# A two-layer hybrid decoder step: the builder orders its instructions by timeline simulation

## The chip, the core and the metric

The kernel runs as one program on one core of a Trainium2 chip. The core has five engines that each work through a fixed list of instructions in order: TensorE (PE; PEld is its weight load), VectorE (DVE), ScalarE (ACT), GpSimd (POOL) and SyncE (SP, which here only issues DMAs). An instruction whose semaphores have not come holds up everything behind it in its engine's list. The metric is the device time of one execution in microseconds (us).

## What is computed

The reference is one inference step of a 2-layer decoder trunk. A prompt of 1024 tokens and eight samples of 8 new tokens each share every weight (d_model 1024, float32).

```python
# layer 0
h = rmsnorm(x); z = h @ w_in0
ya = gated short convolution (conv3) of z[..., :1536]
yb = RWKV-7: token shift, data-dependent decay, delta-rule state update, a step per token
x = x + concat(ya, yb) @ w_out0;  x = x + swiglu(rmsnorm(x))
# layer 1
h = rmsnorm(x); z = h @ w_in1
yc = forgetting attention, causal, with per-token log forget gates; each sample also
     attends to 2048 past rows of a paged K/V cache (page_table)
yd = Mamba-2 SSD: causal conv, chunked scan, gated rmsnorm
x = x + concat(yc, yd) @ w_out1;  x = x + swiglu(rmsnorm(x));  y = rmsnorm(x)
```

The outputs are y and every new state (convolution rows, shift row, WKV state, K, V, log forget gates, SSD state).

## The kernel before

**Halves.** The 1088 tokens (64 of the samples, 1024 of the prompt) are worked in two halves: H0, the samples and the first half of the prompt (576 columns, cut into tiles of 320 and 256), and H1, the second half of the prompt (512 columns). Activations lie with features on partitions. For the last FFN they are regrouped as F0 and F1.

**Dense work.** Every large product is done in three passes to keep float32 accuracy: weight and activation are each split in a rounded high part and a low rest (wh, wl; hh, hl, or hidh, hidl inside the FFN), and `mm3` (L202) issues wh·hh (L204), wh·hl (L205) and wl·hh (L206) into one PSUM accumulator `acc`. `load_w` (L191) brings a weight tile: a DMA of 512 KB on ACT's queue into `wraw`, the cast to wh on ACT (L196), the subtraction to wl on POOL or DVE (L198).

**Side work.** Beside that run three chains of many small steps, each of which goes from PE to DVE, ACT or POOL and back: the RWKV recurrence (L521 to L840: the matmuls L622, L639, L693, L721 and others, many of them 32x32), the attention and decode, and the SSD scan (L1438, L1447). In decode (L1186) each tile of 512 KB of the K cache comes by 8 DMAs on SP's queue (L1245) with addresses taken from the page table, into one of 4 buffers `kv`; DVE transposes it (L1249, into `kt`) and 8 matmuls (L1254) use it. V tiles come by POOL (L1297, matmuls L1290).

**Recording order.** The generators of dense and side work are woven together while the program is recorded:

```python
weave(first(), m.recurrence(H0), RATE[0])    # first: short_conv(H0), project(H1), part of conv H1
weave(second(), m.recurrence(H1), RATE[1])   # second: output product and FFN of H0, layer 0
```

Then the pool of buffers of layer 0 (`m0`) is closed and that of layer 1 (`m1`) opened. The dense part of layer 1 for H0 (`m.dense`, with the gates L987 and their transposition `by_token`, L1061) is recorded, after it `third()` (FFN of H1, dense part of H1) and the FFN of F0, woven with `side` (attention, decode and SSD of H0, then attention and SSD of H1), and last the FFN of F1.

At the opening of `m1` the program loads the constants of layer 1 (L919, L172) and runs `past()` (L1074): the page table, a gather of the past log forget gates (L1088), their running sum on DVE (L1096, L1099), one small matmul over pages (L1101), the result written to DRAM (L1107) and its last column read back into `pcl` (L1109). `by_token` transposes the gates with the matmuls L1067 and L1071; L1067 waits for the DVE copy L1043, L1071 for the DVE subtraction L1046, which reads `pcl`. L919 waits for the buffers of `m0`, that is for L837, the last matmul of the recurrence.

**What sets the order on the chip.** The recorded order is not the executed one. The builder has a scheduler: a model of the machine that steps through time, and at each step gives each engine, of the instructions that its model says are ready, the one recorded first. The lists that come out are fixed; on the chip each engine follows its own list in order, with semaphores between engines. Semaphores, buffers and the number of instructions follow from the program and that order.

## Time and profile before

| | |
|---|---|
| time, median of 3 runs | 3342.44 us (3337.44 to 3342.83) |
| profiled execution | 3342.04 us, span 3340.3 us |
| granted TensorE clock, mean | 0.974 |
| PE busy | 3169.4 us, 95% |
| DVE, ACT, POOL busy | 1906.4, 1058.7, 834.7 us |
| DMA | 409.20 MB, mean 123 GB/s |

PE is busy nearly throughout. Its three dense passes (L204 to L206) make most of it. A PE that counts as busy can still wait between two pipelined matmuls, so the spacing of matmuls tells more than the busy share. The other engines have room on the average; the average runs over stretches that differ, from pure dense work (958 to 1250 us) to stretches where dense and side work alternate.

### The profile page before, as it was taken

Reading aid. Unit: us, or ns where it says so; the run is one execution under the profiler, and the core shown is the slowest. Engines: PE = TensorE matmul, PEld = TensorE weight load, DVE = VectorE, ACT = ScalarE, POOL = GpSimd, SP = SyncE. Lnnn points to the kernel's source line nnn. Section 1 sums busy time; section 2 is a strip of 40 time slices with the busy share of each in tenths; the row PEclk is TensorE's granted clock in tenths of the full one; section 3 lists DMA queues with packets and bytes.
Section 4 is the critical chain, followed back from the end, with each engine's and each line's share of the span. In section 5 each row is a group of like instructions: output and inputs, shape, how many; then the busy total and the mean of one; then the engine's idle time right before and its main releaser. Section 6 shows DMA issues by size and latency. Waiting matters only on the chain. (4 is left out here: it accounts for less than half of the span.)

```text
span 3340.3 us, 63263 instructions
## 1 busy us (share of the span) xinstructions
PE 3169.4 (95%) x25213; PEld 2666.9 (80%) x25213; DVE 1906.4 (57%) x3643; ACT 1058.7 (32%) x2083; POOL 834.7 (25%) x561
## 2 busy tenths in 40 slices
PE   7999999999999998999999998989999998999998
PEld 7887667777889997977677675766777776899998
DVE  6766646565544447556655457565545656554445
ACT  4333323332222223345322223332224553322222
POOL 4423333332333333301300103002010001333332
PEclk9999999999999998999999999999999999999999
DMA  5322333211122234544345656775554334232222
GB/s 178 116 59 79 87 96 118 73 59 56 51 66 83 83 108 148 191 151 135 108 135 163 199 154 213 240 221 175 172 171 138 113 110 135 87 105 81 83 83 78
DMA packets 238471, 409.20 MB, mean 123 GB/s; under 512 B 37632, under 2 KB 129664, under 8 KB 238176
## 3 DMA queue, kind: packets, MB, share of 16 engines
q10 hardware_dynamic: 63232, 218.80, 20.2%
q1 hardware_dynamic: 165584, 152.27, 15.4%
q0 software_dynamic: 9360, 34.08, 3.0%
q8 instruction: 199, 3.26, 0.4%
q14 instruction: 96, 0.79, 0.1%
HBM read 352.23 MB, written 52.81 MB: 121 GB/s over the span
## 5 line engine op out<-in xcount | busy, mean ns | idle before, releaser
L204 PE MATMUL acc<-hh,wh 128*128 128x320 f32 (+2 forms) x3720 | 1264.9, 341 | 17.6 <-ACT hh L218 14.7
L206 PE MATMUL acc<-hh,wl 128*128 128x320 f32 (+2 forms) x3720 | 1255.4, 338 | 7.4 <-POOL wl L198 6.5
L205 PE MATMUL acc<-hl,wh 128*128 128x320 f32 (+2 forms) x3720 | 1254.8, 338 | 7.2 <-DVE hl L219 5.4
L204 PEld LDWEIGHTS acc<-hh,wh 128*128 128x128 f32 x3720 | 712.3, 192 | 97.5 <-ACT hh L218 19.4
L198 POOL TENSOR_TENSOR wl<-wraw,wh 128x1024 fp32r<-128x1024 f32 x225 | 539.6, 2398 | 1000.6 <-ACT wh L196 924.7
L196 ACT CAST wh<-wraw 128x1024 fp32r<-128x1024 f32 (+1 forms) x398 | 416.0, 1045 | 1139.4 <-PE acc L205 1054.1
L206 PEld LDWEIGHTS acc<-hh,wl 128*128 128x128 f32 x3720 | 712.8, 192 | 74.7 <-issue 11.1
L205 PEld LDWEIGHTS acc<-hl,wh 128*128 128x128 f32 x3720 | 713.0, 192 | 72.1 <-DVE hl L219 9.1
L205 PE MATMUL acc<-hidl,wh 128*128 128x320 f32 (+2 forms) x1056 | 353.1, 335 | 0.6 <-DVE hidl L219 0.6
L893 DVE TENSOR_TENSOR x<-x,acc 128x320 f32<-128x320 f32 (+2 forms) x528 | 270.3, 527 | 139.1 <-PE acc L206 136.1
L206 PE MATMUL acc<-hidh,wl 128*128 128x320 f32 (+2 forms) x1056 | 349.5, 332 | 0.0
L204 PE MATMUL acc<-hidh,wh 128*128 128x320 f32 (+2 forms) x1056 | 348.9, 337 | 0.4 <-ACT hidh L218 0.4
L198 DVE TENSOR_TENSOR wl<-wraw,wh 128x1024 fp32r<-128x1024 f32 x173 | 210.9, 1219 | 145.3 <-ACT wh L196 143.2
L1297 POOL DMA_INDIRECT kv<-in_cv,vidx x64 | 75.5, 1180 | 628.8 <-DVE kt L1249 134.4
L204 PEld LDWEIGHTS acc<-hidh,wh 128*128 128x128 f32 x1056 | 198.7, 189 | 24.0 <-issue 4.2
L205 PEld LDWEIGHTS acc<-hidl,wh 128*128 128x128 f32 x1056 | 199.2, 189 | 19.1 <-issue 2.2
L206 PEld LDWEIGHTS acc<-hidh,wl 128*128 128x128 f32 x1056 | 199.5, 189 | 15.6 <-issue 1.4
L219 DVE TENSOR_TENSOR hidl<-ft,hidh 128x512 fp32r<-128x512 f32 (+2 forms) x148 | 178.7, 1207 | 55.9 <-ACT hidh L218 55.8
L881 DVE SCALAR_TENSOR_TENSOR ft<-ft,acc 128x320 f32<-128x320 f32 (+2 forms) x132 | 70.1, 531 | 213.1 <-PE acc L206 212.9
L875 DVE SCALAR_TENSOR_TENSOR ft<-ft,acc 128x320 f32<-128x320 f32 (+2 forms) x132 | 69.7, 528 | 177.0 <-ACT ft L874 176.8
L218 ACT CAST hidh<-ft 128x512 fp32r<-128x512 f32 (+2 forms) x148 | 75.1, 507 | 117.5 <-DVE ft L881 114.3
L1249 DVE STREAM_TRANSPOSE kt<-kv 128x1024 f32<-128x1024 f32 x64 | 79.3, 1239 | 33.8 <-DMA kv<-in_ck 29.9
(339 smaller groups left out, 3334.7 us busy)
## 6 DMA issues: line engine op xcount, KB each, us to landing
wraw<-in_wi ACTq DMA_DIRECT2D x100, 512.0 KB
wraw<-in_wg ACTq DMA_DIRECT2D x88, 512.0 KB
wraw<-in_wu ACTq DMA_DIRECT2D x88, 512.0 KB
wraw<-in_wd ACTq DMA_DIRECT2D x88, 512.0 KB
kv<-in_ck SPq DMA_DIRECT2D x512, 64.0 KB
wraw<-in_wo ACTq DMA_DIRECT2D x32, 512.0 KB
ka<-kp SPq DMA_DIRECT2D x48, 128.0 KB
x<-in_xT SPq DMA_DIRECT2D x16, 288.0 KB
```

Of the source, the lines that this page charges most:

```text
L196: nc.scalar.copy(wh, raw)
L198: k.low.tensor_sub(wl, raw, wh)
L204: mm(acc, wh, xh, start=first, stop=False)
L205: mm(acc, wh, xl, start=False, stop=False)
L206: mm(acc, wl, xh, start=False, stop=last)
L218: k.nc.scalar.copy(hh, v)
L219: (eng or k.nc.vector).tensor_sub(hl, v, hh)
L875: nc.vector.scalar_tensor_tensor(s[:, a:b], s[:, a:b], 1.0, pc, op0=ALU.add, op1=ALU.mult)
L881: nc.vector.scalar_tensor_tensor(s[:, a:b], s[:, a:b], 0.5, pu, op0=ALU.mult, op1=ALU.mult)
L893: nc.vector.tensor_add(xs[n][:, a:b], xs[n][:, a:b], acc[:, :b - a])
L1249: V.transpose(kt, kr)
L1297: nc.gpsimd.indirect_dma_start(out=v, out_offset=None, in_=A["cv"].rearrange("o (s r) c -> (o s) (r c)", r=2), in_offset=bass.IndirectOffs ...
```

## The change

One argument of the context in which the program is recorded:

```diff
-    with tile.TileContext(nc) as tc:
+    with tile.TileContext(nc, schedule_with_timeline_sim=True) as tc:
         hybrid_step(tc, A, O)
```

The scheduler takes another model of the machine, a timeline simulation, to decide which instruction is ready when. No operation is added or removed: there are 20191 matmuls in both programs, and 3643 instructions of DVE. What differs is where they stand in the lists of their engines. PE's list differs most; the start (to about 154 us of the trace), the FFN of H1 and the last FFN stand nearly as before. Three places follow.

**First recurrence, PE.** Before, at the matmul L639 that reads tile t0_3303 (recurrence of H0; t0 and wm are small 32x32 blocks of it, hh and wh the operands of the projection of H1):

```order
L639 MATMUL rk_3305<-t0_3303,nt_2877 32x32 x16
L204 MATMUL acc_3381<-hh_233,wh_3348 128x256
L205 MATMUL acc_3381<-hl_241,wh_3348 128x256
L206 MATMUL acc_3381<-hh_233,wl_3350 128x256
L204 MATMUL acc_3381<-hh_234,wh_3348 128x256
L639 MATMUL rk_3326<-t0_3324,nt_2889 32x32 x16
L205 MATMUL acc_3381<-hl_242,wh_3348 128x256
L206 MATMUL acc_3381<-hh_234,wl_3350 128x256
```

Now, at the same matmul:

```order
L563 MATMUL rk_3300<-sq_3298,con1_259 128x256
L206 MATMUL acc_6859<-hh_6481,wl_6829 128x256
L639 MATMUL rk_3305<-t0_3303,nt_2877 32x32 x16
L639 MATMUL rk_3326<-t0_3324,nt_2889 32x32 x16
L639 MATMUL rk_3407<-tt_3274,wm_3322 32x32 x16
L639 MATMUL rk_3426<-tt_3293,wm_3343 32x32 x16
L693 MATMUL rk_3453<-t0_3450,big_2772 32x32
L693 MATMUL rk_3453<-t0_3450,big_2854 32x32
```

Before, groups of recurrence matmuls and dense passes alternate to the end of the recurrence. Now the dense passes run ahead: the second row is the last of them, and behind it 1274 matmuls of the recurrence follow (376 rows of the list) with no dense pass among them, until the output product of H0 begins.

**Opening of layer 1, PE.** Before, the small matmul of `past()`, L1101 (ptot: totals of the log forget gates of a page), and, more than 500 rows further down, `by_token` (L1067, L1071):

```order
L204 MATMUL acc_15190<-hh_14791,wh_15185 128x320
L205 MATMUL acc_15190<-hl_14799,wh_15185 128x320
L1101 MATMUL rk_15041<-ptot_15039,con3_15016 128x8
L206 MATMUL acc_15190<-hh_14791,wl_15187 128x320
L204 MATMUL acc_15190<-hh_14792,wh_15185 128x320
```

```order
L205 MATMUL acc_15931<-hl_14802,wh_15900 128x256
L206 MATMUL acc_15931<-hh_14794,wl_15902 128x256
L1067 MATMUL acc_15959<-con0_222,x_15148 128x128 x4
L1071 MATMUL acc_15965<-con0_222,x_15148 128x128
L204 MATMUL acc_15978<-hh_14787,wh_15970 128x320
L205 MATMUL acc_15978<-hl_14795,wh_15970 128x320
```

Now the end of the recurrence of H1 (L820, L828, L837) and these matmuls stand together:

```order
L206 MATMUL acc_15931<-hh_14794,wl_15902 128x256
L820 MATMUL rk_11829<-con1_259,s2_11766 128x2 x2
L828 MATMUL rk_11836<-con0_222,s2_11766 128x128 x2
L837 MATMUL rk_11841<-sg_11761,g2_275 128x256
L1067 MATMUL acc_15959<-con0_222,x_15148 128x128 x4
L1101 MATMUL rk_15041<-ptot_15039,con3_15016 128x8
L1071 MATMUL acc_15965<-con0_222,x_15148 128x128
L204 MATMUL acc_15978<-hh_14787,wh_15970 128x320
```

Before, L837 stands some 2800 rows ahead of L1067, and dense passes lie between L1101 and L1067. Now nothing but these few small matmuls stands between L837 and L1071. On SP's list the loads of L919, L172, L1081 and on to L1109 follow directly on the last store of the recurrence, L840.

**Decode, PE.** Before, near the end of the dense part of H1 (kt: a transposed tile of K, qsp: queries; 8 matmuls L1254 use one tile):

```order
L205 MATMUL acc<-hl,wh 128x512
L206 MATMUL acc<-hh,wl 128x512
L1254 MATMUL fs<-kt,qsp 32x128 x8
L204 MATMUL acc<-hh,wh 128x512
L205 MATMUL acc<-hl,wh 128x512
L206 MATMUL acc<-hh,wl 128x512
L1263 MATMUL fs<-ksp,qsp 32x64 x8
L1254 MATMUL fs<-kt,qsp 32x128 x8
L204 MATMUL acc<-hh,wh 128x512
L205 MATMUL acc<-hl,wh 128x512
L206 MATMUL acc<-hh,wl 128x512
```

Now, at the same place of the dense work:

```order
L1311 MATMUL rk<-con_15016,om 64x16 x8
L1254 MATMUL fs<-kt,qsp 32x128 x64
L204 MATMUL acc<-hh,wh 128x512 x2
L205 MATMUL acc<-hl,wh 128x512
L206 MATMUL acc<-hh,wl 128x512
L205 MATMUL acc<-hl,wh 128x512
L206 MATMUL acc<-hh,wl 128x512
L1254 MATMUL fs<-kt,qsp 32x128 x40
L1263 MATMUL fs<-ksp,qsp 32x64 x8
L1254 MATMUL fs<-kt,qsp 32x128 x24
L204 MATMUL acc<-hh,wh 128x512 x2
```

Before, a K tile stands between three or more dense passes. Now 128 matmuls L1254, which is 16 K tiles, stand in a row with six dense passes among them. Before, the recurrence of H1 ends in the first half of the FFN of H0; now it is spread over the whole of it. At the end of the dense part of H1 the last 100 matmuls of the SSD scan of H1 (L1438, L1447 and others) now stand without dense passes as well.

## Rows read from the trace of the kernel before

**Rows 1.** The page: one engine's busy time, and the granted clock in 40 slices.
```profile
PE 3169.4 (95%) x25213; PEld 2666.9 (80%) x25213; DVE 1906.4 (57%) x3643; ACT 1058.7 (32%) x2083; POOL 834.7 (25%) x561
PEclk9999999999999998999999999999999999999999
```

**Rows 2.** Windows: stretch, its length, busy us (records) of each engine, clock, DMA.
```profile
core 0: us, PE busy (x) PEld busy (x) DVE busy (x) ACT busy (x) POOL busy (x), PEclk, DMA share, GB/s
154.00:528.00 374.00, 352.78 (x4702) 269.10 (x4700) 229.55 (x615) 119.43 (x321) 121.09 (x107) 0.96 0.30 87
528.00:958.00 430.00, 401.97 (x4937) 332.20 (x4938) 246.29 (x600) 129.26 (x319) 127.88 (x98) 0.96 0.20 63
958.00:1250.00 292.00, 292.00 (x2163) 289.78 (x2162) 125.37 (x217) 70.66 (x106) 108.20 (x45) 1.00 0.27 89
1520.00:1985.00 465.00, 452.95 (x2548) 335.71 (x2552) 278.39 (x461) 136.64 (x258) 62.93 (x68) 0.98 0.48 148
1985.00:2221.00 236.00, 220.60 (x1341) 160.17 (x1329) 150.49 (x199) 73.39 (x106) 32.30 (x26) 0.97 0.73 221
2221.00:2255.00 34.00, 26.19 (x142) 19.85 (x141) 17.79 (x23) 15.36 (x23) 1.82 (x4) 0.85 0.64 207
2742.00:2832.00 90.00, 79.84 (x414) 61.27 (x413) 63.80 (x133) 35.56 (x74) 16.18 (x11) 0.96 0.36 114
```

**Rows 3.** Waits of PE: us in total, times, longest us.
```profile
PE rk L639 <- DVE wm L660: 8.7, 6, 2.7
```

**Rows 4.** Windows of line L204 alone: length, PE busy (records), PEld, clock, DMA.
```profile
528.00:958.00 430.00, 167.64 (x505) 97.74 (x506) 0.96 0.20 63
254.00:279.00 25.00, 8.43 (x26) 4.88 (x26) 1.00 0.21 64
```

**Rows 5.** Lines by form, PE, 154 to 528 us: count, busy us, mean ns.
```profile
L204 PE MATMUL acc<-hh,wh 128*128 128x512 f32 x136 | 61.2, 450 | 0.0
```

**Rows 6.** Timeline of PE at 2245 us: start us, length us, instruction.
```profile
2244.93 0.39 PE L204 MATMUL acc<-hh,wh 128*128 128x512 f32 x1
2245.17 0.39 PE L205 MATMUL acc<-hl,wh 128*128 128x512 f32 x1
```

**Rows 7.** Windows of 25 us, columns as in rows 2.
```profile
154.00:179.00 25.00, 23.11 (x385) 20.44 (x384) 22.03 (x51) 8.30 (x19) 6.31 (x7) 0.93 0.18 51
254.00:279.00 25.00, 24.57 (x486) 19.83 (x487) 17.23 (x54) 7.63 (x24) 4.70 (x4) 1.00 0.21 64
```

**Rows 8.** Timeline, 1258 to 1370 us, the lines of past() and by_token().
```profile
1260.52 0.33 SPq L919 DMA_DIRECT2D st_conv<-in_st_conv  x1
...
1284.02 0.39 PE L1101 MATMUL rk<-ptot,con 128*128 128x8 f32 x2 [2.35 <-DVE ptot L1099]
1286.62 3.85 SPq L1107 DMA_DIRECT2D ncd<-plf  x8
...
1365.78 0.60 PE L1067 MATMUL acc<-con,x 128*128 128x128 f32 x4
```

**Rows 9.** One line, L1046: duration ns min/median/max, first and last start.
```profile
L1046 DVE TENSOR_TENSOR x<-x,pcl x1: 214/214/214, 1315.2 to 1315.2; 8x64 f32<-8x64 f32 x1
```

**Rows 10.** Timeline, 2139 to 2226 us: transposes of K tiles on DVE.
```profile
2139.60 1.25 DVE L1249 STREAM_TRANSPOSE kt<-kv 128x1024 f32<-128x1024 f32 x1 [6.34 <-DMA kv<-in_ck]
2143.62 1.25 DVE L1249 STREAM_TRANSPOSE kt<-kv 128x1024 f32<-128x1024 f32 x1 [1.01 <-DMA kv<-in_ck]
...
2224.02 1.24 DVE L1249 STREAM_TRANSPOSE kt<-kv 128x1024 f32<-128x1024 f32 x1
```

**Rows 11.** Timeline of SP, the same stretch: K loads.
```profile
2161.76 27.28 SPq L1245 DMA_DIRECT2D kv<-in_ck  x32
```

**Rows 12.** Chain of waits, 2815 to 2850 us: start us, us, what.
```profile
2822.49 1.17 PE rk L255 x8
...
2831.24 4.70 DMA ft<-yb
...
2836.01 0.68 ACT hh L218
```

## The prediction

> **What bounds the kernel now.** The page comes first. PE is busy 3169.4 of 3340.3 us and its granted clock stands near 1 in all slices [rows 1], so PE sets the time, and the change leaves PE's instructions as they are. What an order can change is how long PE waits, how long it runs at the lower of its two clock levels (1.2 against 2.4 GHz), and how long work of another engine lies with nothing for PE beside it. The windows by stage show how these differ now [rows 2]. From 958 to 1250 us PE has dense passes alone: 292.0 busy of 292 us, clock 1.00, 2163 matmuls, so 0.135 us for one of 320 or 256 columns. From 154 to 528 and from 528 to 958 us the two recurrences run beside dense work. There PE is idle 21.2 and 28.0 us and the clock is 0.96. The waits behind it are many and short: the longest sum of such a pair, L639 for wm, is 8.7 us in 6 times, none over 2.7 [rows 3]. The stretch 2221 to 2255, where the K tiles of decode get dense, is the worst by share: 7.8 of 34 us idle, clock 0.85 [rows 2].
>
> So the kernel before is bounded by PE, with a few per cent lost in many small waits. The question for a new order is what it saves of these and whether it makes long ones. Five terms follow, each the new time of a stretch less its time before.
>
> **1. First recurrence, 154 to 528 us.** Before, 374 us [rows 2]. This stretch holds 913 dense passes and 1942 matmuls of the recurrence (counted in the order). A dense pass of 512 columns comes every 0.24 us, start to start [rows 6]; 3 x 136 = 408 are of this kind [rows 5], and the other 505 cost 0.135 each: 98 + 68 = 166 us. The recurrence thus took 208 us of PE's time, 0.107 us a matmul, with all its waits.
> Now the dense passes run ahead. Beside them lie 668 of the 1942; at 0.107 that is 71, with half of the waits gone about 55, so the mixed part takes 221 us. Then 1274 matmuls run alone, and the time of that is the time of the chain through the other engines. In DVE's list 358 instructions lie beside them. At the mean of this stretch, 229.55 / 615 = 0.373 us [rows 2], that is 134 us of work: the lower bound, DVE full. The upper one is DVE's share of this stretch, 61%: 218 us. The stretch with the busiest DVE did 51 instructions in 25 us [rows 7], which makes 175, and I take this, since without dense passes in between PE answers sooner than on the mean. Behind the recurrence comes a tail that dense work covered before: result to DRAM, back, split. The same chain at the end of layer 1 goes from 2822.5 to 2836.0 [rows 12], 13.5 us with a norm; I take 10. Sum 221 + 175 + 10 - 374 = **+32** (ends 208 + 134 + 5 and 237 + 218 + 13.5: -27 to +95).
>
> **2. Second recurrence, 528 to 1250 us.** Now it is spread over the whole FFN of H0, so that between two links of its chain about twice as much dense work lies. What can go is the idle time, 28.0 us, and the low clock, 0.04 of 402 = 16: 44 us, the lower end. The upper end goes by the pace of the side matmuls: the stretch holds 3 x 505 = 1515 dense passes [rows 4], 204 us at 0.135, which leaves 226 us for 3422 records of side matmuls, 66 ns each. In the best 25 us of the first recurrence (486 records, 79 of them dense, clock 1.00 [rows 4, 7]) the same sum gives 35 ns, and 31 ns x 3422 = 106. I take the middle, since the small waits that a busy PE hides should shrink but small matmuls keep a price: **-75** (-106 to -44).
>
> **3. Opening of layer 1.** Before, the loads begin at 1260.5 (L919), the page sums reach PE at 1284.0 (L1101), go to DRAM from 1286.6 (L1107), and L1046 ends at 1315.4 [rows 8, 9]: a chain of 54.9 us. by_token, which needs it, came only at 1365.8 [rows 8], and dense passes filled PE all the while. Now L1071 stands a few matmuls behind L837, and the chain cannot begin before L837, since L919 waits for it. Behind L1071 the whole of PE's list waits, and with it the weight loads that reuse buffers and the casts. Nothing hides the chain any more. DVE and the queues are quieter than before, which I put at 5 us: **+50** (+40 to +57).
>
> **4. Decode, 1520 to 2255 us.** Now 16 K tiles come at the end with six dense passes. Before, twelve K tiles were transposed between 2139.6 and 2224.0, 7.7 us apart, the closest 4.0 [rows 10]; SP issued 32 of their loads in 27.3 us, 6.8 us for a tile of eight [rows 11]. With three tiles already in the 4 buffers, 13 are waited for, at 7.0 us each 91 us, and about 15 us of other PE work is in the stretch that took 34 before [rows 2]: +72. Against this the 12.1 + 15.4 us of idle time and the low clock (about 16 us) of 1520 to 2221 [rows 2] shrink where the tiles are fewer, by 25: **+47** (-14 at 4.0 us a tile with all of 43 gained, +104 at 7.7 a tile of 16 and nothing gained).
> The Trainium skill (DMA: Bandwidth & Descriptors, section Issuing engines are not separate DMA queues) says that starting a DMA takes the sequencer a time that is usually small relative to the transfer itself. By that rule the tiles would come at the rate of the transfers: 8.4 MB at the 221 GB/s that the queues moved in 1985 to 2221 [rows 2] is 38 us in place of 91, and the sum would be 53 us less. Rows 11 speak against it: 32 loads of 64 KB in 27.3 us are 77 GB/s from this queue.
>
> **5. SSD of H1, 2742 to 2832 us.** Before, 90 us with about 219 dense passes in it, some 50 us at the prices above, so the scan took 40 us of PE's time. Now it runs alone: not under 40, not above the 90 it took with its neighbours; DVE was busy 63.8 there, dense work included [rows 2]. I take 55, and 13 for the tail, which now nothing covers [rows 12]: 55 + 13 - 40 = **+28** (+5 to +63).
>
> **Sum.** 32 - 75 + 50 + 47 + 28 = +82 us. Against the profiled execution (3342.04 us, that is 0.4 us under the median of the runs) this makes 3424 us. The rest of the span, 0 to 154 us, the FFN of H1 and the last FFN, has nearly the same order and stays.
>
> **Rivals.**
> (a) *The lone chains are quick*: 3322 us. In the mix each link of a chain waited in PE's list behind dense passes that were ahead of it; alone it goes at the pace of DVE and of SP. Then term 1 is at DVE's share in the busiest stretch, 22.03 of 25 us [rows 7]: 134 / 0.88 = 152, so 208 + 152 + 8 - 374 = -6; term 3 is +40; term 4 has 4.0 us a tile, 52 + 15 - 34 - 25 = +8; term 5 +13; with -75 the sum is -20. It decides when the lone recurrence takes under about 150 us and a tile about 4. For it speaks the tile pair 4.0 us apart; against it that the busiest stretch shows fewer instructions than its share would have it, and all the terms must go the same way. The transfer rule above would lead here too. Chance 0.14.
> (b) *The lone chains run at the low clock*: 3530 us. PE is idle for most of a lone stretch, and in rows 2 the clock is lower where PE has been idle more (0.85 in 2221 to 2255). At 1.2 GHz the 1274 matmuls of term 1, at 35 ns a record and two records each, take 89 us more, all of it in the chain, and the scan of term 5 up to 20. Against it: the chain waits for DVE more than for PE, so the matmuls' length counts only once a link. Chance 0.13.
> (c) *No change*: 3342. PE's work is the same, and small waits go as long ones come; terms 2 and 3 to 5 would have to cancel to 7 us. Only an accident does that: 0.04.
> My own case has 0.69.
>
> **How the numbers follow.** The likeliest is 3424. Its own range: the ends of the five terms lie 60, 31, 9, 59 and 29 us from their middles, and as they are independent they add to about 95, so 3345 to 3510. On the lower side the range is taken down to 3330, to hold half of (a); above it ends at 3505, which leaves out most of (b). About 2 in 10 lie outside. A measurement of this kernel can tell about 0.2%, 7 us, from no change. Faster by more than this is most of (a) and a small part of my own case, 0.14; within it (c) and the edge of the others, 0.05; slower 0.81.
>
> **What would show it.** In the profile after: (1) a stretch of 130 to 220 us from about 370 us on with L639, L721 and others on PE and no L204, PE's busy share well under 0.7, and waits for DVE (wm, t, S) and ACT there; the dense part ahead of it without waits. (2) The FFN of H0 with PE near 100% and the clock near 1.00 while the recurrence runs. (3) One wait of PE of some 45 to 50 us at L1067, L1101 and L1071 together. (4) PE waiting for kt (L1249) tile by tile, about 7 us apart, for around 100 us, with SP issuing K loads without pause. (5) L1438 and L1447 alone for 45 to 70 us, then a wait for ft of about 10 us. The prediction is wrong if the lone recurrence is done in under 140 us or the K tiles come at under 5 us; it is wrong on the other side if the granted clock in these stretches is near 0.5 and their matmuls double. If the spread of the second recurrence saves nothing, the time goes up by another 75 us.

## The result and the profile after

The changed kernel takes 3496.52 us (median of 4 runs, 3491.76 to 3503.11); the kernel before, on the same chip, 3342.64 us. The ratio is 1.0459, 95% interval 1.0446 to 1.0472: slower by 154 us. That is within the range on record, near its upper end, and nearly twice the rise of 82 us that the likeliest case had.

The page of the kernel after, the lines that answer to [rows 1]:

```profile
PE 3198.3 (91%) x25213; PEld 2723.4 (78%) x25213; DVE 1935.6 (55%) x3643; ACT 1069.2 (31%) x2083; POOL 842.2 (24%) x561
PEclk9999666999999998899999999859999997899999
```

PE's busy time is nearly the same; the span grew by 161 us, and the granted clock has four dents: 350 to 613 us, 1313 to 1488, 2188 to 2363 and 2888 to 3063. Only the second had a counterpart before, one slice at 8 [rows 1]. The windows show what lies there (columns as in [rows 2]):

```profile
153.00:364.00 211.00, 209.69 (x2214) 178.69 (x2214) 119.16 (x264) 69.53 (x138) 80.65 (x50) 1.00 0.37 112
364.00:583.00 219.00, 174.37 (x2493) 128.79 (x2492) 117.12 (x346) 53.99 (x184) 39.95 (x57) 0.63 0.17 48
583.00:1090.00 507.00, 500.49 (x4970) 459.23 (x4971) 276.13 (x580) 150.02 (x305) 184.79 (x107) 0.99 0.24 76
1090.00:1381.00 291.00, 278.22 (x2818) 255.27 (x2817) 156.65 (x302) 92.49 (x186) 103.09 (x58) 0.96 0.32 102
1381.00:1415.00 34.00, 3.06 (x11) 1.87 (x11) 13.23 (x26) 1.47 (x3) 2.21 (x4) 0.50 0.31 86
2000.00:2245.00 245.00, 233.27 (x1414) 166.84 (x1413) 153.50 (x204) 79.44 (x115) 39.75 (x38) 0.99 0.76 237
2245.00:2342.00 97.00, 23.46 (x318) 13.41 (x316) 26.82 (x28) 4.03 (x6) 3.70 (x4) 0.53 0.46 133
2926.00:3006.00 80.00, 55.72 (x350) 50.85 (x350) 45.62 (x108) 28.46 (x60) 17.95 (x11) 0.78 0.37 112
3006.00:3481.00 475.00, 455.63 (x3355) 451.23 (x3354) 220.69 (x359) 119.89 (x185) 173.98 (x75) 0.98 0.24 79
```

All four lone places of the prediction are there. From 153 to 364 us PE runs the dense passes of the first stretch with hardly a gap. From 364 to 583 the recurrence is alone: PE busy 174 of 219 us at clock 0.63, DVE 117. From 1381 to 1415 PE does almost nothing. From 2245 to 2342 the K tiles stand alone, from 2926 the scan of H1. The FFN of H0, on the other hand, is nearly full: 500.5 of 507 us at 0.99, where the kernel before had 402 of 430 at 0.96 beside the same recurrence [rows 2].

The waits of PE that changed, in total over the span (us, times, longest us); that for kt as it was before stands in the second fence:

```profile
PE fs L1254 <- DVE kt L1249: 84.1, 27, 6.9
PE acc L1071 <- DVE x L1046: 14.8, 1, 14.8
PE acc L1067 <- DVE x L1043: 9.5, 1, 9.5
PE acc L204 <- DVE x L893: 8.4, 12, 0.8
PE rk L639 <- DVE wm L660: 8.1, 8, 1.6
PE rk L1101 <- issue: 6.6, 1, 6.6
```

```profile
PE fs L1254 <- DVE kt L1249: 7.9, 6, 3.7
```

The wait for wm, the longest of the recurrence before [rows 3], has hardly shrunk in total. Before, 8.4 of its 8.7 us stood in the first recurrence; now 5.0 of 8.1 stand in the lone stretch of that recurrence.

The next table is worked out: eight matmuls were taken as borders, the start of the same matmul was looked up in both traces, and the differences are those of the two profiled executions (3342.04 and 3503.11 us). The first border is the fifth L622, the second the first L204 of the output product of H0, the last the end of the last FFN's dense passes.

| stretch, us in the trace before | before, us | after, us | difference | term on record |
|---|---|---|---|---|
| 153.9 to 528.0 | 374.1 | 430.1 | +56.0 | 1: +32 |
| 528.0 to 1379.0 | 851.0 | 845.6 | -5.4 | 2 and 3: -25 |
| 1379.0 to 1520.4 | 141.4 | 148.0 | +6.6 | none |
| 1520.4 to 2254.9 | 734.5 | 785.3 | +50.8 | 4: +47 |
| 2254.9 to 2531.9 | 277.1 | 286.6 | +9.5 | none |
| 2531.9 to 2857.5 | 325.6 | 356.7 | +31.1 | 5: +28 |
| 2857.5 to 3318.7 | 461.2 | 475.2 | +14.0 | none |

The wait at the opening of layer 1, on PE and SP (`...` marks lines left out):

```profile
1380.74 1.06 PE L837 MATMUL rk<-sg,g 128*128 128x256 f32 x2
1384.39 0.34 SPq L919 DMA_DIRECT2D st_conv<-in_st_conv  x1
...
1391.30 1.11 PE L1067 MATMUL acc<-con,x 128*128 128x128 f32 x4 [9.50 <-DVE x L1043]
1399.05 0.57 PE L1101 MATMUL rk<-ptot,con 128*128 128x8 f32 x2 [6.64 <-issue]
...
1414.42 0.48 PE L1071 MATMUL acc<-con,x 128*128 128x128 f32 x1 [14.80 <-DVE x L1046]
```

The chain that took 54.9 us beside dense work [rows 8, 9] takes 30.0 from L919 to L1071 with nothing beside it. And the lone K tiles, on DVE and on SP:

```profile
2278.26 1.25 DVE L1249 STREAM_TRANSPOSE kt<-kv 128x1024 f32<-128x1024 f32 x1 [4.11 <-DMA kv<-in_ck]
2283.56 1.25 DVE L1249 STREAM_TRANSPOSE kt<-kv 128x1024 f32<-128x1024 f32 x1 [4.05 <-DMA kv<-in_ck]
2288.79 1.25 DVE L1249 STREAM_TRANSPOSE kt<-kv 128x1024 f32<-128x1024 f32 x1 [3.98 <-DMA kv<-in_ck]
```

```profile
2244.36 42.73 SPq L1245 DMA_DIRECT2D kv<-in_ck  x64
```

A tile every 5.3 us here, 5.8 on the mean of all 16, each waited for by DVE. SP issues without pause: 64 loads in 42.73 us, 0.67 us for one. Within it two loads in a row start 0.51 us apart, and reading the address of the next page, once for four loads, takes another 0.6. The first load leaves at 2244.4, when the lone stretch begins, so none of the 16 tiles lay ready. It could not leave earlier: K and V tiles share the 4 buffers `kv`, and SP waited for V tiles and the matmuls that read them (SP's waits, 2200 to 2300 us):

```profile
SPq L1245 <- DMA kv<-in_cv,vidx: 23.5, 1, 23.5
SPq L1245 <- PE rk L1290: 4.5, 1, 4.5
```

### The profile page after: what moved, and what is told of

It reads as the page before. It is cut to its first block, busy times and chain, and to the rows that moved or that the text cites. A ratio compares the mean times of both kernels' runs of the same rounds, so it can differ in the third digit from the quotient of the medians.

```text
span 3501.3 us, 63255 instructions
## 1 busy us (share of the span) xinstructions
PE 3198.3 (91%) x25213; PEld 2723.4 (78%) x25213; DVE 1935.6 (55%) x3643; ACT 1069.2 (31%) x2083; POOL 842.2 (24%) x561
## 5 line engine op out<-in xcount | busy, mean ns | idle before, releaser
L204 PE MATMUL acc<-hh,wh 128*128 128x320 f32 (+2 forms) x3720 | 1246.8, 337 | 33.5 <-ACT hh L218 22.1
L206 PE MATMUL acc<-hh,wl 128*128 128x320 f32 (+2 forms) x3720 | 1246.9, 336 | 2.9 <-POOL wl L198 2.3
L204 PEld LDWEIGHTS acc<-hh,wh 128*128 128x128 f32 x3720 | 711.0, 192 | 103.7 <-ACT hh L218 26.6
L206 PEld LDWEIGHTS acc<-hh,wl 128*128 128x128 f32 x3720 | 711.4, 191 | 67.9 <-issue 6.6
L204 PE MATMUL acc<-hidh,wh 128*128 128x320 f32 (+2 forms) x1056 | 341.6, 338 | 8.6 <-DVE x L893 8.4
L206 PE MATMUL acc<-hidh,wl 128*128 128x320 f32 (+2 forms) x1056 | 347.7, 331 | 0.0
L893 DVE TENSOR_TENSOR x<-x,acc 128x320 f32<-128x320 f32 (+2 forms) x528 | 267.3, 528 | 142.4 <-PE acc L206 140.5
L204 PEld LDWEIGHTS acc<-hidh,wh 128*128 128x128 f32 x1056 | 197.3, 188 | 37.3 <-DVE x L893 12.3
L206 PEld LDWEIGHTS acc<-hidh,wl 128*128 128x128 f32 x1056 | 198.9, 189 | 15.5 <-issue 0.3
L219 DVE TENSOR_TENSOR hidl<-ft,hidh 128x512 fp32r<-128x512 f32 (+2 forms) x148 | 167.0, 1129 | 51.3 <-ACT hidh L218 51.0
L1254 PE MATMUL fs<-kt,qsp 128*32 128x128 f32 x1024 | 48.2, 314 | 84.1 <-DVE kt L1249 84.1
```

What stands on the lines that cost most here:

```text
L204: mm(acc, wh, xh, start=first, stop=False)
L206: mm(acc, wl, xh, start=False, stop=last)
L219: (eng or k.nc.vector).tensor_sub(hl, v, hh)
L893: nc.vector.tensor_add(xs[n][:, a:b], xs[n][:, a:b], acc[:, :b - a])
L1254: mm(ps[r0:r0 + 32, 128 * g:128 * g + 128], qsp[:, 2 * e + u, 2 * bp + c].rearrange("p a q -> p (a q)"), k4[c][:, :, 2 * e + u], start=u = ...
```

## Experiments

Each was run with the kernel before on the same chip. A difference from the kernel before is that of the medians of these runs; one from the changed kernel goes by the two ratios to the kernel before, since they were not run together. Two models had to be told apart at first: either the four lone places are the loss and can be taken away one at a time, or the order as a whole costs, in whatever place.

**Tying the dense passes to the first recurrence.** In the changed kernel:

```diff
-            weave(first(), m.recurrence(H0), RATE[0])
+            weave(first(), m.recurrence(H0), RATE[0], tie=(tc, 100))
...
+        with tie[0].issue_after(sent[-1 - tie[1]]) if tie and len(sent) > tie[1] else nullcontext():
+            try:
+                next(dense)          # sent: matmuls of the side, as recorded
```

> The changed kernel with one constraint more: beside the first recurrence each dense step may be issued only behind the recurrence matmul that was recorded about 100 matmuls earlier, so the dense part cannot run ahead and the 1274 matmuls no longer stand alone. Theory (the lone stretch costs the time: 430 us in the trace from the first recurrence matmul L622 to the output product against 374 before, with a granted clock of 0.63 in its second half): 40 to 60 us go, 3437 to 3457 us, and no long stretch at a low clock is left there. Rival (the stretch is bounded by the chain of the recurrence itself, and ties only turn waits of the chain into waits of dense passes): the time stays within 15 us of 3497.

Measured: 3519.45 us, ratio to before 1.0550 (1.0529 to 1.0572). That is 0.9% or 30 us slower than the changed kernel (ratio 1.0459) in place of 40 to 60 faster, and the rival, that it stays within 15 us, missed too. The lone stretch is gone, but the whole stretch takes 444 us:

```profile
154.00:598.00 444.00, 383.13 (x4710) 305.39 (x4708) 234.84 (x611) 121.46 (x321) 120.01 (x107) 0.84 0.25 76
```

PE is idle 61 us, in many places, at clock 0.84. The tie gives the dense passes in lumps, and between two lumps the chain stands alone for a while, with the same result in smaller pieces. So the theory, as it was put, fell: this tie does not cure the place by keeping dense work back.

**by_token behind the convolution products**, in the changed kernel:

```diff
-        self.by_token(H, rw)
         for i in (4, 5, 6, 7, 0, 1, 2, 3):
             self.conv(H, h, i)
             yield
+        self.by_token(H, rw)
```

> The changed kernel with by_token recorded behind the eight convolution products of the dense part instead of ahead of them. Theory (PE's wait at the opening of layer 1, 34 us from L837 to L1071, is the chain of loads, gather and page sums, which has only to be covered by dense work): 30 to 42 us less, 3455 to 3467 us, the low clock behind the wait included. Rival (the wait moves: another load of the opening, or the buffers that the convolution needs, holds PE at the same place): no more than 10 us less.

Measured: 3476.22 us, ratio 1.0422 (1.0399 to 1.0445): 12 us less than the changed kernel by the ratios, 20 by the medians, between the two. The wait itself is gone. Of PE's waits for this chain only that for ptot is left, and the window from 1370 to 1440 us has PE idle 7.8 us, where the changed kernel has 34.9 (second fence):

```profile
PE rk L1101 <- DVE ptot L1099: 2.9, 1, 2.9
```

```profile
1370.00:1440.00 70.00, 35.12 (x237) 33.33 (x237) 34.45 (x63) 12.85 (x28) 13.59 (x10) 0.71 0.49 149
```

So 27 us went at the place, and from the total 12 by the ratios, with an interval of about 3 to 21. Part of it came back just behind: between the borders of the table the stretch 528 to 1379 fell from 845.6 to 803.0 us, and the next one rose from 148.0 to 161.7.

**Tying the dense passes to attention, decode and scan**, in the changed kernel: the same tie, 30 matmuls, on the two weaves of layer 1 with `side`.

> The changed kernel with the constraint in layer 1 only: each dense step of the FFN of H1, its dense part and the FFN of F0 may be issued only behind the attention, decode or scan matmul recorded about 30 matmuls earlier. 16 K tiles no longer stand in a row and the scan of H1 no longer runs alone. Theory (the lone K tiles, 97 us at clock 0.53, cost 51 us net and the lone scan 31): 60 to 85 us less, 3412 to 3437 us. Rival (the K tiles are bound by SP, which issues them one after another at 0.67 us a load, wherever they stand): the wait for kt stays at about 84 us in sum and the time falls by under 30 us.

Measured: 3535.36 us, ratio 1.0585 (1.0560 to 1.0610): 1.3% or 42 us slower than the changed kernel. Between the same two matmuls the stretch with the lone K tiles fell from 117 to 32.5 us, and the wait for kt from 84.1 to 19.4 us. But the three stretches around it (1379 to 1520, 1520 to 2221 and 2255 to 2532 us of the trace before) grew by 40, 45 and 45 us, with waits that were not there before:

```profile
PE fs L1254 <- DVE kt L1249: 19.4, 4, 13.1
PE fs L1155 <- ACT s L1164: 16.6, 11, 4.4
PE rk L1290 <- DMA kv<-in_cv,vidx: 14.4, 8, 4.0
PE rk L1174 <- DVE s L1168: 13.9, 11, 3.4
```

Neither theory nor rival: the K tiles can be hidden, but a tie pays for it elsewhere.

**All three.**

> The three edits together. Theory (the loss is the sum of the three lone places, and what the timeline order gains elsewhere, about 39 us in the second recurrence, is kept): 3497 less 50, 36 and 72 is 3339 us, so level with the kernel before or a little under it. Rival (each tie puts back the short waits of the kernel before, or the places share a cause so that the gains overlap): 3380 us or more.

Measured: 3515.88 us, ratio 1.0529 (1.0506 to 1.0551). The rival's side: the ties put waits back. After these four runs the question was turned round: not to take pieces of the loss away, but to put pieces of the change into the kernel before.

**A lone recurrence in the kernel before.** The old scheduler model, and only the rate of the first weave changed, so that 1101 matmuls of the recurrence stand behind the last dense pass:

```diff
-RATE = (5.5, 6, 1.8, 1.8, 1)
+RATE = (1.9, 6, 1.8, 1.8, 1)
```

> The kernel before (its own scheduler model) with the first weave's rate 1.9 in place of 5.5, so that the recurrence is recorded late and 1101 of its matmuls stand behind the last dense pass, as in the changed kernel, while everything else keeps the order of before. Theory (the lone stretch itself costs, in whatever order its parts stand): 40 to 60 us more than before, 3380 to 3400 us, with a granted clock of 0.6 to 0.7 in the stretch. Rival (the timeline order of DVE, ACT and POOL inside the recurrence is what costs, which would also explain why tying the dense passes to the recurrence saved nothing): not over 15 us more, under 3355.

Measured: 3398.47 us, ratio 1.0175 (1.0158 to 1.0192), 57 us more than before. The lone stretch:

```profile
390.00:587.00 197.00, 152.56 (x2144) 112.91 (x2142) 102.12 (x303) 47.06 (x156) 40.51 (x56) 0.61 0.17 50
```

From the last dense pass to the output product these are 197 us for 1101 matmuls, where the changed kernel has 219 for 1274: the same pace and as low in clock (0.61 and 0.63), with an order of its steps that the old model made. The lone stretch by itself costs what term 1 lost. (The clocks of 0.68 and 0.86 in the expectations below are means from 354 us on, and take in 36 us of mixed work at 1.00.)

**The same with extra dense passes in the lone stretch** (the rest of the kernel is whole, their result is unused):

```diff
+            with tc.issue_after(new[-1]):      # behind every fifth, or tenth, recurrence matmul
+                tc.nc.tensor.matmul(acc, h[0][0][:, 0:128], h[0][1][:, 0:512], start=True, stop=True)
```

> The same, and in the lone stretch one extra dense pass of 512 columns (0.21 us at the full clock, its result unused) behind every fifth recurrence matmul, some 220 to 230 passes or about 50 us of PE work. Theory (the low clock lengthens the lone chain: 174 us of PE busy at 0.63 in place of some 117): the clock stays near 1.00 and the stretch is not longer than without the passes, so the time is between 20 us under and 5 us over that of the kernel without them. Rival (the chain goes through DVE and ACT and the clock matters little): the passes stand in the chain's way and add 20 to 50 us.

> The kernel before with the recurrence recorded late (3398 us, clock 0.68 in the lone stretch) and one extra dense pass of 512 columns, result unused, behind every tenth recurrence matmul: some 115 passes, about 25 us of PE work, half of the run before (3430 us, clock 0.86). Theory (the low clock makes a good part of the lone stretch: the 50 us of passes there added only 32): the clock rises to 0.75 or more and the time is at most 8 us over the run without passes, 3390 to 3406 us. Rival (every pass stands in the chain's way at its full price): 16 to 30 us over it, 3414 to 3428 us.

Measured: 3430.11 us with every fifth (ratio 1.0263, 1.0237 to 1.0288), 32 us over the run without; 3410.58 us with every tenth (1.0202, 1.0183 to 1.0221), 12 us over it by the medians and 9 by the ratios, since these two were not run together. The stretch, with every tenth and every fifth:

```profile
391.00:600.00 209.00, 173.57 (x2266) 123.38 (x2264) 104.31 (x307) 46.27 (x159) 40.92 (x57) 0.74 0.17 48
```

```profile
390.00:610.00 220.00, 191.97 (x2422) 137.45 (x2421) 105.98 (x309) 46.07 (x158) 40.79 (x57) 0.84 0.16 46
```

The clock rose from 0.61 to 0.74 and 0.84, and the stretch did not become shorter: 115 and 231 passes, some 28 and 55 us of added work at the 0.24 us of [rows 6], made it 12 and 23 us longer. So more than half of the added work is paid for, by the idle time of PE (44 us without, 35 and 28 with) and by the faster clock. An estimate parts the two: PE's busy time grew by 21 and 39 us for 28 and 55 of work, so the other matmuls took some 7 and 16 us less. The first run came out as its rival had it, the second between the two. What is shown: a higher clock, bought with extra passes, does not rescue a lone chain. How much shorter the stretch would be at the full clock without extra work stays open.

**The spread alone**, in the kernel before:

```diff
-RATE = (5.5, 6, 1.8, 1.8, 1)
+RATE = (5.5, 3, 1.8, 1.8, 1)
```

> The kernel before with the second weave's rate 3 in place of 6: the recurrence of H1 is spread over the FFN of H0 about as in the changed kernel, but ends some 100 us ahead of by_token, so there is no wait at the opening of layer 1. Theory (spreading ends the short waits; the changed kernel gained about 39 us there): 30 to 55 us less than before, 3285 to 3310 us. Rival (the gain comes from the timeline order and not from the spread): within 10 us of before.

Measured: 3343.35 us, ratio 1.0006 (0.9994 to 1.0017): nothing. The rival was right: spreading the second recurrence over the FFN does not end the waits.

**The change in three parts.** The kernel before and its model, and the lists of PE, DVE, ACT and POOL held to the changed kernel's order for one part of the program:

```diff
         hybrid_step(tc, A, O)
+        keep_order(tc, RUNS)     # RUNS: numbers of the instructions, by engine, in the order wanted
...
+                if prev is not None:
+                    tc.add_manual_dep(i, prev, mybir.DependencyInfo(mybir.DependencyClass.NoSync, mybir.DependencyReason.DATA), reason="keep_order")
+                prev = i.name
```

> The kernel before and its scheduler model, with the lists of PE, DVE, ACT and POOL held to the order of the changed kernel for the work recorded up to the first recurrence's end (start, short convolution, projections, recurrence of H0), and nothing else held. Theory (the change is the sum of independent parts; here the segment from L622 to the output product grew from 374 to 430 us): 50 to 62 us more than before, 3391 to 3403 us. Rival (parts interact: what is lost here was gained later, by work that had run ahead): under 3375 us.

> The same, held to the changed kernel's order only for the output product and FFN of H0 with the recurrence of H1 and the conv of H1. The recurrence then ends some 47 us of dense work ahead of by_token, so the wait at the opening of layer 1 is mostly covered. Theory (the timeline order leaves about 2.4 us of dense passes between two side matmuls in place of 0.5, and PE no longer waits: 448.6 of 450 us busy in the changed trace at clock 1.00 against 426 of 450 here before): 35 to 50 us less than before, 3291 to 3306 us. Rival (as in the run that only spread the recurrence, nothing is gained): within 10 us of before.

> The same, held to the changed kernel's order only for layer 1 and all that follows. The recurrence ends 350 us of dense work ahead, so the loads of layer 1 start early; L1101, L1067 and L1071 stand together as in the changed kernel. Theory (segments of the two traces: +7, -32, +83, +10, +31, +14 us): 105 to 140 us more, 3446 to 3481 us, the upper end if the chain from L1101 to L1071 still makes PE wait about 25 us. Rival (the losses of layer 1 are made by the late recurrence and its late loads, not by layer 1's own order): not over 60 us more.

| part held to the new order | us | ratio to before, interval | difference |
|---|---|---|---|
| up to the end of the first recurrence | 3398.07 | 1.0177 (1.0156 to 1.0197) | +59 |
| FFN of H0 with the second recurrence | 3318.87 | 0.9940 (0.9920 to 0.9959) | -20 |
| layer 1 and the rest | 3486.19 | 1.0441 (1.0416 to 1.0466) | +148 |

The first part has the lone stretch of the changed kernel in nearly all its numbers (compare the second window above):

```profile
364.00:584.00 220.00, 176.07 (x2527) 131.52 (x2525) 120.05 (x352) 54.78 (x184) 40.74 (x59) 0.64 0.17 49
```

The middle part gains, though 20 us and not the 35 to 50 expected, and where: the run that only spread the recurrence, and the one with the new order, in the same 450 us:

```profile
650.00:1100.00 450.00, 428.50 (x4556) 390.43 (x4555) 246.11 (x530) 123.61 (x277) 142.80 (x90) 0.98 0.21 66
```

```profile
650.00:1100.00 450.00, 448.57 (x4696) 417.59 (x4695) 246.22 (x531) 128.78 (x271) 157.73 (x93) 1.00 0.23 74
```

Both have the recurrence spread; only the second has no waits. The new order keeps more dense passes between two side matmuls. Counted in PE's lists, from the output product of H0 to L837, a run of dense passes between two side matmuls has a median of 4 passes before and 21 after; in the first recurrence 3 before and 19 after. In the traces of the two runs shown here it is 5 with the spread alone and 19 with the new order. That this distance is what ends the waits is argued from these counts: the lists of DVE, ACT and POOL were held together with PE's, and no run parts them. The last part costs more than the 140 us at the upper end of its theory, and makes PE wait as the changed kernel does:

```profile
PE fs L1254 <- DVE kt L1249: 97.2, 25, 8.7
...
PE acc L1071 <- DVE x L1046: 15.1, 1, 15.1
PE acc L1067 <- DVE x L1043: 9.5, 1, 9.5
```

although the recurrence ends as early there as in the kernel before, and the loads (L919) leave at 1257.5 us, over 100 us ahead of L1101 at 1366.9. What the chain waited for in between is the order of layer 1's own steps on ACT and POOL: L926, the first small step of layer 1 on ACT, and the gather L1088 on POOL start only at 1357.4 and 1357.9, behind the casts and splits of the dense work, and DVE stands for L926:

```profile
1357.68 0.51 DVE L1032 TENSOR_SCALAR x<-x,an 8x576 f32<-8x576 f32 x1 [25.53 <-ACT an L926]
1357.93 1.34 POOL L1088 DMA_INDIRECT plf<-in_clf,pidx  x1 [0.17 <-issue]
```

On PE, L1101 and L1071 follow directly. So the wait at the opening is made by the order of layer 1's own steps, and not by the late end of the recurrence. The middle part is the counterpart: there the recurrence ends late and layer 1 has its old order, and PE waits 8.6 us at L1101 and not at L1067 or L1071. The three parts sum to +187 us and the change is +154. Some 15 us of the difference lie in layer 1 after 1520 us; SP's list was not held there, but that this is the reason is not shown, and the rest is not settled.

**The middle part with by_token late.**

> The kernel before with the changed kernel's order held for the output product and FFN of H0 with the recurrence of H1 (as in the run that held this part alone, 3319 us), and by_token recorded behind the convolution products. That run still waited 8.6 us at L1101 and had PE idle 6 to 7 us in 50 at clock 0.83 to 0.96 between 1200 and 1340 us. Theory (this is the same chain of past() and the gates, which needs only cover): 8 to 20 us less than that run, 3299 to 3311 us. Rival (the loss there is the start of layer 1 itself, its first weight tiles and the norm, as in the kernel before): within 6 us of 3319.

Measured: 3320.05 us, ratio 0.9930 (0.9912 to 0.9948). The intervals of this run and of the middle part overlap: by_token is worth nothing there, as the rival had it. The wait that the theory was after, 8.6 us at L1101, is still there (8.8): L1101 belongs to `past()`, and the edit moved only `by_token`. Both are the fastest kernels of the study, 0.6 to 0.7% under the kernel before.

## Why the prediction was right, and where its terms were off

The direction and the reason held. Slower because long lone stretches replace many short waits: the run with the lone recurrence in the old model and the first part show it for the recurrence, and the last part with its waits for layer 1. But the sum was half of what came, and the time lies 8 us inside the upper end: the range held because it was wide. Two of its sums were off besides. The lower end of term 4 comes to -10 and not -14 by its own figures, and 3424 with 95 to either side is 3329 to 3519, not 3345 to 3510. The terms were right in different degrees.

*Term 1, +32 on record, +56 measured* (+57 and +59 in the two runs that had this part alone). The mixed part was priced well: 221 on record, 211 in the trace. The term that was mis-sized is the lone chain: 175 us by the pace of the busiest 25 us [rows 7], with 10 for the tail, against 219 with it. DVE was busy 117 of these 219 us, 53%, under the 61% of the upper bound. The busiest window of a mix was the wrong neighbour: there the steps of the recurrence and those of the short convolution (L365, L369) filled DVE together. Alone no engine was full: PE 80% busy at the low clock, DVE 53%, ACT 25%. And "without dense passes in between PE answers sooner" brought little: from the last L838 (the end of a round on DVE) of the first round to that of the last round the chain took 250 us in the mix (270.2 to 520.6), with 513 dense passes in it, and 201 alone (375.6 to 576.7).

*Term 2, -75 on record; -20 in the run that has this part alone, and some -39 in the changed kernel (the -5.4 of the table less the 34 of the opening).* The price of a side matmul record was taken as 44 ns. In the middle part it is 46: 873 + 874 + 873 = 2620 dense passes from 650 to 1100 us (lines L204 to L206) at 0.135 are 354 us, and 96 are left for 2076 records. So the place is as full as it was thought, but its ends are not: from 528 to 650 PE is idle 9.5 us at clock 0.94, from 1100 to 1379 17.2 at 0.94, where the kernel before has 8.1 and 12.1 at 0.97, and 19.9 from 650 to 1100. So the idle time fell by 12 us in all, where the forecast began at 28 with 16 more for the clock. And the reason given was wrong. "Twice as much dense work" between two links does nothing by itself, as the spread alone showed; it takes the new order, in which a run of dense passes between two side matmuls is about five times as long.

*Term 3, +50: 34 us without work for PE, and 12 to 20 us gained when it was covered.* The chain was priced at 54.9 less 5; without dense work beside it, it took 30.0. The 54.9 us were no measure of the chain: in that trace DVE did the gates' steps (L1003 to L1042) ahead of L1046, which began 0.03 us after L1042 ended, and SP took 9.9 us over the loads of L1109, with other stores ahead of them, where it took 5.3 alone. And the step "the chain cannot begin before L837" was right for the changed kernel but not the cause, as the last part showed.

*Term 4, +47 on record, +51 measured*, by errors that cancel. A tile came every 5.8 us and not 7.0, but 16 tiles were waited for and not 13, 93 us for 91; the stretch that had 34 us before took 117, +83 in place of +72, and 1520 to 2221 gave back 32 in place of 25. That three tiles would lie ready was wrong, since V tiles held the buffers. SP's issuing set the pace, as the prediction had it. The Trainium skill (DMA: Bandwidth & Descriptors, Issuing engines are not separate DMA queues) calls the time to start a DMA usually small relative to the DMA itself. In this stretch it was not: 0.67 us a load on SP while the core moved 133 GB/s, against 237 in the stretch ahead of it, at which 64 KB would take an estimated 0.28 us.

*Term 5, +28 on record, +31 measured.* The agreement is luck. The lone scan took 39 us and not 55 (2926.5 to 2965.5), the tail to the next L204 16 and not 13; these 55 us in place of 68 came to +31 because only 24 went elsewhere and not the 40 taken off.

*The rest, 0 on record, +30 measured.* The last FFN was taken as unchanged and grew by 14 us, with eleven waits of L204 for the DVE addition L893, 8.0 us in sum, that it did not have; two stretches of layer 1 grew by 7 and 10. The prediction put this at nothing on the ground that PE's order is nearly the same there. Term 1 (24 us), terms 2 and 3 together (20) and this rest (30) make nearly all of the missing half.

Rival (a), quick lone chains, fell on the recurrence: 219 us against its mark of 150. A tile, at 5.3 to 5.8 us against 4.0, lay between it and the 7.0 of the likeliest case. Rival (b), the lone chains at the low clock, was right about the clock (0.63, 0.53, 0.78 in the lone windows), and its total of 3530 us is nearer to the result than the likeliest case; but its price, 89 us in term 1, is not borne out: the estimate above has the faster clock giving back some 16 us at 0.84, and passes that raised the clock did not shorten the stretch. Rival (c) fell.

The shape of the whole is simpler than the terms. The new model leaves about five times as many dense passes between two links of a chain. Where there is dense work enough, from 528 to 1379 us before (4439 passes for 1765 side matmuls), PE hardly waits, and the part by itself gains 20 us. Where there is not, in the first recurrence (913 passes for 1942), the passes are used up after a third of the chain, and what is left stands alone.

## What to carry to other kernels

Before believing that an order hides a chain better, count how much covering work there is and how much the order spends per link: what is spent early is missing at the end, and a chain left alone ran here with no engine full. The Trainium skill (Perfetto Trace Analysis, Optimization Strategy) says that interleaving stretches with different limits may improve the time; the lone recurrence agrees, at 57 us lost without it. A scheduler's model need not be taken or left as a whole: holding its order for the one part where it fits gave 0.6% here, where the whole cost 4.6%.

## What the runs showed of the hardware

- A chain of loads, a gather and small DVE steps took 54.9 us beside dense work and the gates' steps, and 30.0 alone: in the mix nearly half of the time it stood behind other work in the lists of DVE and SP.
- The granted clock of a stretch in which PE is 80% busy (176 of 220 us) with small matmuls and many short waits was 0.64 in the run of the first part, a mean over its two levels (1.2 and 2.4 GHz); in the changed kernel the stretch ahead, 99% busy with dense passes in it, had 1.00. In the kernel before with a lone recurrence, extra dense passes raised it from 0.61 to 0.84.
- Loads of 64 KB with register addresses left SP every 0.67 us when nothing held them up (0.51 from one to the next, and 0.6 more for a page's address, once for four loads), and every 0.85 us beside dense work and its weight loads [rows 11].
